# Copies of the key tiles issued from ScalarE's queue, and the key transposes at a higher scheduling priority

## The chip, the cores and the metric

The kernel runs on one core of one Trainium2 chip. The metric is the device time in microseconds (us) of one execution; lower is better. A core has five engines that run their own instruction streams side by side: PE (TensorE, matrix multiplications and transposes), DVE (VectorE), ACT (ScalarE), POOL (GpSimd) and SP (SyncE, which here only issues transfers). Transfers (DMAs) are issued by an instruction on one of these streams and then run by themselves; an instruction that needs the data waits for a semaphore. Each stream is in order: an instruction that waits holds back all that stand behind it on its engine.

## The reference

One step of a two-layer streaming encoder, on 1024 new frames of one stream ("prompt", 8 tiles of 128 rows) and on 8 running streams of 16 frames ("sample", one tile of 128 rows), model width 1024, 16 query heads and 4 key heads of 64.

```python
for layer in range(DEPTH):                       # DEPTH = 2
    if layer < N_LAYERS_A:                       # layer 0, mixer A
        qp, kp, vp = project_a(hp, g_attn[layer], w_qkv_a[i], g_q_a[i], g_k_a[i])
        ap = band_attention_prompt(qp, kp, vp, LEFT_CHUNKS_A, alibi_fn, sink_a[i])
        ...                                      # the same for the sample, with cached keys
        hp = hp + ap @ w_o_a[i]
    else:                                        # layer 1, mixer B
        kb_p, vb_p = shared_kv(hp, g_kv, w_kv, g_k_b)
        qp = project_q_b(hp, g_attn[layer], w_q_b[j], g_q_b[j])
        ap = band_attention_prompt(qp, kb_p, vb_p, LEFT_CHUNKS_B, rel_fn, None)
        ...
        hp = hp + ap @ w_o_b[j]
    hp = hp + mlp(hp, g_mlp[layer], w_up[layer], w_down[layer])
    hs = hs + mlp(hs, g_mlp[layer], w_up[layer], w_down[layer])
```

project_a and shared_kv are an RMS norm, a projection and an RMS norm of each key head; attention is softmax(q k^T + bias) v over the own 64-row chunk and 2 (A) or 8 (B) chunks before it; the MLP is relu(x w_up)^2 w_down.

## The kernel before

Every fp32 matrix product is made of values that are split in two, hi and lo, and three matmuls (L186 to L188 in the projections, L147 to L149 in the output projection, L715 to L717 in the MLP). A split is a cast on ACT (L109, hi) and a subtraction on DVE (L115, lo).

In each layer an attention part is followed by an output projection and an MLP. The attention part handles the 8 prompt tiles t = 0..7 and the sample tile ST. For one tile these steps are called, each a small function in the code:

- X(t): the tile's input is loaded from DRAM, x<-xd in layer 1 (L1319, issued by SP).
- N(t): eight PE transposes (ps_n, L179), the split into hh and hl, the sum of squares on ACT (junk, L170). For most tiles hh and hl are also stored to DRAM (hTd, L1349); R(t) brings them back later for the other projection chunks (hh<-hTd, hl<-hTd, L1358). There is one pair of buffers for hh and hl.
- K1(t): the key and value projection, and its finish kv_stage1 (kw by ACT L252 and L253, the norm, ks on DVE).
- K2(t): k_transpose. Two PE transposes of ks into a PSUM tile ps_q (L229), a split into the key tile KT[:, t, :, 0] (two casts on ACT, two subtractions on DVE, of 64 partitions each), and then two DMAs (L282 and L283, 64 partitions and 128 KB each) that copy the two halves, exchanged, into KT[:, t, :, 1]. Scores take a query's upper or lower half against a key tile in the same partitions, so both copies are needed (matmuls L349 in layer 0, L400 and L468 in layer 1).
- Q1(t, nb) and Q2(t, nb): the query projection, its norm (qn and qr on ACT, L195 and L196), four PE transposes of qr into ps_q (L229), and the split into qT (L109 and L115).
- Scores, softmax (L354 to L385 in layer 0, L428 to L440 and L486 in layer 1), transposes of p (ps_tr, L293), their split pth and ptl, and the product with the values (ps_pv, L300 and L301).

Eight prompt tiles in two layers make 16 calls of k_transpose with copies, and so 32 DMAs.

The code calls these steps in the order of a plan, but the order in which they stand on each engine is set by the framework's scheduler: it takes the instructions by priority (those recorded earlier have the higher one) against its own simulation of the engines. `with self.tc.high_priority(n)` raises the priority of what is recorded inside it by n. Both the instruction stream of ACT and that of SP are a result of that scheduling, and so are buffers' reuse and who waits for whom. Nothing is written out by hand here (cfg's `order` is empty).

Each DMA, when it ends, raises one of eight semaphores (DMAHW0 to DMAHW7), which all hardware DMAs of SP and ACT take in turn; before a DMA is issued, its engine waits until the earlier DMA on the same semaphore has landed.

Of the kernel before, what the change touches and what calls it, by code (L numbers as in the profile page):

```python
# [8 lines left out]
F32 = mybir.dt.float32  # L9
# [66 lines left out]
class Build:  # L76
# [197 lines left out]
    def k_transpose(self, ks, dst):  # L274
        a, b = slice(0, 64), slice(64, 128)
        pt = self.transpose_pairs(ks, 2)
        even, odd = dst[0][:, 0::2], dst[0][:, 1::2]
        self.split(even[a], even[b], pt[a])
        self.split(odd[b], odd[a], pt[b])
        if len(dst) > 1:  # L280
            if self.kd:
                self.nc.sync.dma_start(dst[1][a].bitcast(F32), dst[0][b].bitcast(F32))  # L282
                self.nc.sync.dma_start(dst[1][b].bitcast(F32), dst[0][a].bitcast(F32))  # L283
            else:
                even, odd = dst[1][:, 0::2], dst[1][:, 1::2]
                self.split(even[b], even[a], pt[a])
                self.split(odd[a], odd[b], pt[b])
# [324 lines left out]
    def wo_phase(self, layer, sx, x8, wo):  # L612
        nc = self.nc
        with ExitStack() as st:
# [6 lines left out]
            def O(t, z):  # L621
# [8 lines left out]
                if t in self.wo_done:  # L630
                    return
                with self.tc.high_priority(WO_PRIO) if len(osp) < 2 else nullcontext():
                    load_o(t, z)
# [5 lines left out]
            def load_o(t, z):  # L639
                o = work.tile([P, 4, P], F32, tag=f"o{z}", name="o")  # L640
                self.load_halves(layer, 1, t, o, second, nc.vector)
                oh = work.tile([P, 4, P], F32R, tag=f"oh{z}", name="oh")
                ol = work.tile([P, 4, P], F32R, tag=f"ol{z}", name="ol")
                self.split(oh, ol, o)
                osp[t] = oh, ol
# [73 lines left out]
    def behind(self, a, b):  # L719
        self.tc.add_manual_dep(b.ins, a.ins.name, AFTER, reason="order")  # L720

# [540 lines left out]
    def attention(self, layer):  # L1262
# [17 lines left out]
        with ExitStack() as st:  # L1280
# [24 lines left out]
            hts, qTs, qss, kss, probs, oTs, xr = {}, {}, {}, {}, {}, {}, {}  # L1305
# [74 lines left out]

            def K2(t):
                if t < NT:
                    self.k_transpose(kss.pop(t), [self.KT[:, t, :, v] for v in range(2)])
                else:
                    kt8 = self.rawp.tile([P, KV, P], F32R, tag="raw", name="kt8")
                    self.k_transpose(kss.pop(t), [kt8])
                    nc.sync.dma_start(self.kT8d[layer], kt8.bitcast(F32))
# [203 lines left out]
            spill(0)  # L1591
            run(Q1(0, 0))
            K2(0)
            spill(1)
            run(Q1(1, 0, "s"))
            Q2(0, 0)
            K2(1)
            spill(ST)
            run(Q1(ST, 0, "s"))
            K2(ST)  # L1600
            X(2)
            N(2)
# [57 lines left out]
            for s in range(2 * NT):  # L1660
# [8 lines left out]
                a, b, c, d = cfg["up"]  # L1669
# [72 lines left out]
]  # L1742

WO_PRIO = 600
AFTER = mybir.DependencyInfo(mybir.DependencyClass.NoSync, mybir.DependencyReason.DATA)
EARLY = (300, 150, 110, 90)
WO_ORDER = [[0, 4, 1, 5, 2, 6, 3, 7, ST], [0, 4, 1, 5, 6, 2, 7, 3, ST]]
# [51 lines left out]
```

## Time and profile before

| | us |
|---|---|
| median of 3 runs | 2405.27 |
| lowest and highest | 2404.04, 2407.24 |
| span of the profiled execution | 2399.3 |
| PE busy | 2320.4 (97% of the span) |
| DVE busy | 1626.3 (68%) |
| ACT busy | 1217.9 (51%) |
| POOL busy | 535.6 (22%) |

The profiled execution has a span, from its first to its last recorded instruction; no other time is listed for it, so it is the span that stands beside the median of the runs, which is 6.0 us longer. A row of a timeline gives the start, the duration, the engine, the line, the operation, the tile written and the tile read, and in brackets how long the engine sat idle before it and what ended that wait. "SPq" and "ACTq" are the issues of DMAs on SP and ACT. The attention part of layer 0 lies at about 43 to 283 us of the span, that of layer 1 at about 1184 to 1391 us.

### The profile page before, as it was taken

How to read it: one execution, taken by the hardware profiler on the slowest of the kernel's cores; microseconds unless marked ns; L12 is line 12 of the kernel's file. 1: busy time of each engine (PE TensorE's matmuls, PEld its weight loads, DVE VectorE, ACT ScalarE, POOL GpSimd, SP SyncE). 2: the span in 40 equal slices, each digit the busy share in tenths (PEclk: the TensorE clock that was granted, in tenths of full speed). 3: DMA queues.
4: the chain of work that ended last, by engine and by line, in shares of the span. 5: the costliest groups of instructions: out<-in, count | busy, mean ns of one | idle time of the engine just before them, and what ended most of it. 6: DMA issues, size and time to landing. Idle time of an engine off the chain costs nothing.

```text
span 2399.3 us, 33421 instructions
## 1 busy us (share of the span) xinstructions
PE 2320.4 (97%) x11621; PEld 1935.5 (81%) x11621; DVE 1626.3 (68%) x3002; ACT 1217.9 (51%) x2423; POOL 535.6 (22%) x828
## 2 busy tenths in 40 slices
PE   7998999899999999999999999998999999999999
PEld 6786877788888888888777788887888888888887
DVE  6687786755655777776567877877655555776674
ACT  4676675555555433232267666665655555333321
POOL 3343332312112100000333434344211211000000
PEclk9998999999999999999999999999999999999999
DMA  7345546244433874342743555555434435744332
GB/s 244 122 127 168 171 156 200 95 155 158 145 128 141 323 245 146 117 141 99 237 149 111 188 161 173 173 169 174 138 127 145 154 137 200 278 140 158 112 116 114
DMA packets 218457, 385.88 MB, mean 161 GB/s; under 512 B 50408, under 2 KB 125104, under 8 KB 211120
## 3 DMA queue, kind: packets, MB, share of 16 engines
q1 hardware_dynamic: 195136, 307.16, 39.0%
q0 software_dynamic: 21776, 71.84, 7.7%
q10 hardware_dynamic: 1376, 4.74, 0.5%
q8 instruction: 92, 1.51, 0.3%
q14 instruction: 77, 0.63, 0.1%
HBM read 246.47 MB, written 136.14 MB: 159 GB/s over the span
## 4 chain that ended last, share of the span: by engine, by line
PE 82%; DMA 7%; DVE 5%; ACT 2%; issue 2%; POOL 1%; SPq 1%; ACTq 0%; DVEq 0%; POOLq 0%
PE ps_x L715 9%; PE ps_x L717 9%; PE ps_x L716 9%; PE ps_y L717 7%; PE ps_y L716 7%; PE ps_y L715 7%; PE ps_mm L186 3%; PE ps_mm L188 3%; PE ps_mm L187 3%; PE ps_tr L293 2%; PE ps_mm L147 2%; PE ps_mm L149 2%; PE ps_mm L148 2%; PE ps_s L717 1%; PE ps_s L716 1%
## 5 line engine op out<-in xcount | busy, mean ns | idle before, releaser
L109 ACT CAST w<-r 128x2048 fp32r<-128x2048 f32 x56 | 107.1, 1913 | 322.9 <-PE ps_y L717 212.1
L715 PE MATMUL ps_x<-w,s 128*128 128x512 f32 x512 | 199.5, 390 | 2.7 <-DVE hc L854 2.1
L717 PE MATMUL ps_x<-w,s 128*128 128x512 f32 x512 | 199.4, 389 | 0.0
L716 PE MATMUL ps_x<-w,s 128*128 128x512 f32 x512 | 199.2, 389 | 0.0
L186 PE MATMUL ps_mm<-w,hh 128*128 128x512 f32 x432 | 175.0, 407 | 13.8 <-ACT kw L253 5.1
L188 PE MATMUL ps_mm<-w,hl 128*128 128x512 f32 x432 | 174.3, 403 | 1.7 <-DMA hl<-hTd 1.4
L187 PE MATMUL ps_mm<-w,hh 128*128 128x512 f32 x432 | 172.5, 400 | 0.7 <-DVE w L159 0.7
L109 ACT CAST s<-s 128x2048 fp32r<-128x2048 f32 x56 | 107.1, 1913 | 117.9 <-DMA s<-hd 108.6
L115 DVE TENSOR_TENSOR w<-r,w 128x2048 fp32r<-128x2048 f32 x56 | 128.2, 2290 | 51.9 <-ACT w L109 51.9
L715 PE MATMUL ps_x<-sx,w 128*128 128x512 f32 (+1 forms) x408 | 157.8, 387 | 4.6 <-ACT hc L834 2.7
L1021 DVE TENSOR_TENSOR x<-ps_y,x 128x512 f32<-128x512 f32 x136 | 92.3, 687 | 101.1 <-PE ps_y L717 101.0
L717 PE MATMUL ps_x<-sx,w 128*128 128x512 f32 (+1 forms) x408 | 154.1, 378 | 0.0
L716 PE MATMUL ps_x<-sx,w 128*128 128x512 f32 (+1 forms) x408 | 154.1, 378 | 0.0
L109 ACT CAST w<-ru 128x512 fp32r<-128x512 f32 (+1 forms) x160 | 110.0, 708 | 85.3 <-PE ps_y L716 32.0
L717 PE MATMUL ps_y<-w,s 128*128 128x512 f32 x384 | 149.5, 389 | 0.0
L716 PE MATMUL ps_y<-w,s 128*128 128x512 f32 x384 | 149.4, 389 | 0.0
L715 PE MATMUL ps_y<-w,s 128*128 128x512 f32 x384 | 149.4, 389 | 0.0
L115 DVE TENSOR_TENSOR s<-s 128x2048 fp32r<-128x2048 f32 x56 | 128.1, 2287 | 26.5 <-ACT s L109 26.5
L115 DVE TENSOR_TENSOR ptl<-ps_tr,pth 128x512 fp32r<-128x512 f32 x180 | 122.6, 685 | 24.8 <-ACT pth L109 19.0
L115 DVE TENSOR_TENSOR w<-ru,w 128x512 fp32r<-128x512 f32 (+1 forms) x160 | 126.6, 793 | 10.9 <-ACT w L109 10.8
L109 ACT CAST pth<-ps_tr 128x512 fp32r<-128x512 f32 x180 | 104.8, 594 | 47.9 <-PE ps_tr L293 39.3
L115 DVE TENSOR_TENSOR wq<-ru,wq 128x1024 fp32r<-128x1024 f32 x32 | 39.7, 1240 | 131.9 <-ACT wq L109 131.9
(280 smaller groups left out, 6573.3 us busy)
## 6 DMA issues: line engine op xcount, KB each, us to landing
s<-hd SPq DMA_DIRECT2D x56, 1024.0 KB, 4.7
ru<-in_w_up SPq DMA_DIRECT2D x64, 512.0 KB, 3.9
r<-in_w_down SPq DMA_DIRECT2D x32, 1024.0 KB, 5.7
hd<-hc POOLq DMA_DIRECT2D x128, 256.0 KB, 2.7
hd<-hs POOLq DMA_DIRECT2D x96, 256.0 KB, 2.5
x<-xd SPq DMA_DIRECT2D x41, 512.0 KB, 4.6
o<-oTd SPq DMA_DIRECT2D x52, 256.0 KB, 4.1
hTd<-hh SPq DMA_DIRECT2D x36, 256.0 KB, 4.5
```

What stands on the lines that cost most here:

```text
L109: a = nc.scalar.copy(hi, src)
L115: return a, e.tensor_tensor(lo, src, hi.bitcast(F32), ALU.subtract)
L147: nc.tensor.matmul(ps, oh[:, k, :], w[:, 0, k, nn], start=(k == 0), stop=False)
L148: nc.tensor.matmul(ps, oh[:, k, :], w[:, 1, k, nn], start=False, stop=False)
L149: nc.tensor.matmul(ps, ol[:, k, :], w[:, 0, k, nn], start=False, stop=(k == 3))
L186: nc.tensor.matmul(ps, a, w[:, 0, k, :], start=(k == 0), stop=False)
L187: nc.tensor.matmul(ps, a, w[:, 1, k, :], start=False, stop=False)
L188: nc.tensor.matmul(ps, b, w[:, 0, k, :], start=False, stop=(k == KC - 1))
L715: a = mm(ps, ah, bh, start=first, stop=False, skip_group_check=True)
L716: mm(ps, ah, bl, start=False, stop=False, skip_group_check=True)
L717: return a, mm(ps, al, bh, start=False, stop=last, skip_group_check=True)
L1021: tt(xs[t][:, N[n]], ps, xs[t][:, N[n]], ALU.add)
```

## The change

The two copies in k_transpose are issued by ACT (nc.scalar) instead of SP (nc.sync), and the call of k_transpose for the prompt tiles stands inside high_priority(100), which raises the priority of its transposes, of its casts and subtractions, and of its two DMAs. Lines after L1382 stand one lower in the changed code.

```diff
@@ k_transpose
         if len(dst) > 1:
             if self.kd:
-                self.nc.sync.dma_start(dst[1][a].bitcast(F32), dst[0][b].bitcast(F32))
-                self.nc.sync.dma_start(dst[1][b].bitcast(F32), dst[0][a].bitcast(F32))
+                self.nc.scalar.dma_start(dst[1][a].bitcast(F32), dst[0][b].bitcast(F32))
+                self.nc.scalar.dma_start(dst[1][b].bitcast(F32), dst[0][a].bitcast(F32))
@@ attention part
             def K2(t):
                 if t < NT:
-                    self.k_transpose(kss.pop(t), [self.KT[:, t, :, v] for v in range(2)])
+                    with self.tc.high_priority(K_PRIO):
+                        self.k_transpose(kss.pop(t), [self.KT[:, t, :, v] for v in range(2)])
@@
 WO_PRIO = 600
+K_PRIO = 100
```

Both parts change what the scheduler makes of the attention parts: instructions change places on all five engines between 48 and 282 us and between 1184 and 1390 us of the old span, and at a few places between 346 and 373 us. The MLPs and most of the output projections keep their order. SP loses 32 rows and ACT gains them.

Three places follow. The first is on SP at the start of layer 1, where x<-xd_113 is the input of a prompt tile; the two pairs of KT copies are those of tiles 0 and 1.

```order
 L265 DMA out<-v_11058 128x256
 L1349 DMA hTd_128<-hl 128x512
-L282 DMA KT<-KT 64x4x128
-L283 DMA KT<-KT 64x4x128
 L263 DMA out<-kw 128x256
-L282 DMA KT<-KT 64x4x128
 L1319 DMA x<-xd_113 128x1024
-L283 DMA KT<-KT 64x4x128
-L1387 DMA kT8d_158<-kt_11465 128x512
+L1388 DMA kT8d_158<-kt_11465 128x512
 L1319 DMA x<-xd_114 128x1024
```

Between the store of kw and the load of x<-xd_113 nothing is left on SP.

On ACT at the same place, before, the casts of tile 1's keys and queries alternate:

```order
L195 ACTIVATE qn<-ps_mm 128x512
L196 COPY qr<-ps_mm 128x512
L109 CAST qT<-ps_q 64x4x128
L109 CAST KT<-ps_q 64x2x128
L109 CAST qT<-ps_q 64x4x128
L109 CAST KT<-ps_q 64x2x128
L195 ACTIVATE qn<-ps_mm 128x512
```

And after:

```order
L195 ACTIVATE qn<-ps_mm 128x512
L196 COPY qr<-ps_mm 128x512
L109 CAST KT<-ps_q 64x2x128
L109 CAST qT<-ps_q 64x4x128
L109 CAST KT<-ps_q 64x2x128
L282 DMA KT<-KT 64x4x128
L283 DMA KT<-KT 64x4x128
L109 CAST qT<-ps_q 64x4x128
L195 ACTIVATE qn<-ps_mm 128x512
```

The second cast of qT now stands behind both issues.

The second place is on ACT in layer 0 at tile 1 (about 52 us), before:

```order
L109 CAST qT<-ps_q 64x4x128
L109 CAST KT<-ps_q 64x2x128
L195 ACTIVATE qn<-ps_mm 128x512
L170 ACTIVATE junk,xssq<-x 128x1024
L109 CAST qT<-ps_q 64x4x128
L109 CAST kt_644<-ps_q 64x2x128
L109 CAST KT<-ps_q 64x2x128
```

And after:

```order
L109 CAST KT<-ps_q 64x2x128
L196 COPY qr<-ps_mm 128x512
L109 CAST qT<-ps_q 64x4x128
L109 CAST KT<-ps_q 64x2x128
L282 DMA KT<-KT 64x4x128
L109 CAST qT<-ps_q 64x4x128
L195 ACTIVATE qn<-ps_mm 128x512
L109 CAST kt_644<-ps_q 64x2x128
L170 ACTIVATE junk,xssq<-x 128x1024
L283 DMA KT<-KT 64x4x128
```

The long junk instruction has moved behind the second cast of qT, and one DMA issue has come ahead of that cast.

The third place is on PE in layer 0 near tile 6 (about 175 us), where hh_2409 and hl_2410 are a pair that R(t) brings back from DRAM, before:

```order
L188 MATMUL ps_mm_2313<-w_352,hl_2061 128x512
L349 MATMUL ps_s_2339<-KT_214,qT_2235 128x256
L574 MATMUL ps_utp_2320<-identr_66,sp_2165 128x128
L575 MATMUL ps_utp_2320<-identr_66,sp_2165 128x128
L293 MATMUL ps_tr_2326<-identr_66,p_2034 128x128 x4
L300 MATMUL ps_pv_2358<-pth_2288,VS_215 128x512
L301 MATMUL ps_pv_2358<-ptl_2289,VS_215 128x512
L576 MATMUL ps_utp_2320<-identr_66,pn_2163 128x128
L186 MATMUL ps_mm_2581<-w_2396,hh_2409 128x512
```

And after, where the same ps_utp group stands:

```order
L186 MATMUL ps_mm_2581<-w_2396,hh_2409 128x512
L349 MATMUL ps_s_2422<-KT_214,qT_2235 128x256 x4
L187 MATMUL ps_mm_2581<-w_2396,hh_2409 128x512
L188 MATMUL ps_mm_2581<-w_2396,hl_2410 128x512
L574 MATMUL ps_utp_2320<-identr_66,sp_2165 128x128
L575 MATMUL ps_utp_2320<-identr_66,sp_2165 128x128
L293 MATMUL ps_tr_2326<-identr_66,p_2034 128x128
L576 MATMUL ps_utp_2320<-identr_66,pn_2163 128x128
L293 MATMUL ps_tr_2326<-identr_66,p_2034 128x128 x3
```

The whole projection of 24 matmuls into ps_mm_2581, which needs the reload, has come ahead of the group.

The DMAs on ACT and SP take the eight semaphores in one common turn, so an issue on ACT can have to wait for a transfer of SP. In the changed program most of the 32 issues share theirs with a store or a small load from the tile before; in layer 0 the second issue for tile 7 shares it with the load hl<-hTd that SP issued at 194.45 us of the old span, and behind that issue on ACT stand the softmax steps L382 and the casts of pth.

## The prediction

> **What bounds the kernel now.** I read the page's first lines, then the stretches of the span, then the waits of PE, SP and ACT, and then the timelines of the places that the change touches.
>
> ```profile
> span 2399.3 us, 33421 instructions
> PE 2320.4 (97%) x11621; PEld 1935.5 (81%) x11621; DVE 1626.3 (68%) x3002; ACT 1217.9 (51%) x2423; POOL 535.6 (22%) x828
> ```
>
> PE is busy for 97% of the span: the kernel is bound by matmuls, and no more than 79 us of idle PE are left in all. What a change of queues and of order can win is part of that, and the half-speed clock that follows some of it. The view of busy time by stretch tells where it lies (columns: stretch, its length, busy time and instructions of PE, PEld, DVE, ACT and POOL, then the mean granted PE clock, the DMA share and GB/s).
>
> ```profile
> 43.00:283.00 240.00, 221.79 (x1194) 182.98 (x1193) 185.36 (x599) 162.12 (x472) 94.56 (x163) 0.96 0.46 146
> 480.00:1184.00 704.00, 700.40 (x3278) 585.08 (x3277) 445.75 (x507) 293.38 (x367) 80.79 (x144) 1.00 0.48 167
> 1184.00:1391.00 207.00, 193.72 (x1032) 157.49 (x1032) 157.47 (x439) 137.53 (x373) 84.30 (x112) 0.99 0.52 158
> 55.00:60.00 5.00, 4.78 (x17) 3.58 (x16) 4.23 (x13) 4.38 (x12) 0.89 (x2) 0.66 0.69 228
> 1209.00:1214.00 5.00, 4.97 (x25) 4.21 (x26) 2.46 (x12) 4.02 (x14) 2.74 (x7) 0.66 0.53 164
> ```
>
> The MLP of layer 0 (480 to 1184) leaves 3.6 us idle and is not changed. The two attention parts, where the change acts, leave 240 - 221.79 = 18.2 and 207 - 193.72 = 13.3 us. ACT works 162.12 + 137.53 of 447 us there, 67%, so it has room, but it is no empty engine. The last two rows are short stretches behind two waits of PE: the clock is 0.66 over 5 us, so each holds 0.34 x 5 = 1.7 us of lost speed beside the wait itself.
>
> **Part 1: SP loses 32 issues.** The operations' own views and SP's waits:
>
> ```profile
> L282 SPq DMA_DIRECT2D KT<-KT x16: 597/617/707, 42.2 to 1377.2; - x16
> L655 ACTq DMA_DIRECT2D xd<-x x9: 326/327/373, 407.4 to 1673.5; - x9
> SPq L282 <- ACT KT L109: 20.4, 8, 5.7
> ```
>
> A copy costs SP 0.617 us of issue (minimum, median and maximum in ns), so 32 x 0.617 = 19.7 us leave SP. SP bounds nothing by its issues; the 19.7 us are worth nothing by themselves. What counts is the third row: SP stood 20.4 us in 8 waits at the first copy, for ACT's cast of KT, the longest 5.7 us, and whatever was queued behind stood too. I looked for the place where that reached PE.
>
> ```profile
> 1197.79 0.35 SPq L263 DMA_DIRECT2D out<-kw  x1
> 1203.91 0.60 SPq L282 DMA_DIRECT2D KT<-KT  x1
> 1204.60 0.55 SPq L1319 DMA_DIRECT2D x<-xd  x1
> 1205.25 0.60 SPq L283 DMA_DIRECT2D KT<-KT  x1
> 1203.87 1.91 PE L400 MATMUL ps_sn<-KT,qT 128*128 128x128 f32 x12
> 1208.90 1.20 PE L179 MATMUL ps_n<-identr,x 128*128 128x128 f32 x8 [3.13 <-DMA x<-xd]
> 1204.60 4.26 DMA x<-xd
> 1203.03 0.58 ACT L109 CAST qT<-ps_q 64x512 fp32r<-64x512 f32 x1 [0.55 <-DVE qT L115]
> ```
>
> SP issues a store at 1197.79, stands until 1203.91 for the cast, and only then issues the load of x, which lands 4.26 us later (the row of the chain) at 1208.9. PE had nothing else: 3.13 us idle, and 1.7 us by the clock, 4.8 us in all. After the change the load follows the store at once: issue at about 1198.2, landing at 1202.5, before PE is through with its scores. But on ACT the second cast of qT (1203.03 before) now stands behind two issues, 2 x 0.617 = 1.2 us, and the scores L400 need it. So the wait for x goes, and about 1.4 us of waiting for qT takes its place: 3.13 - 1.4 = 1.7 us of idle time saved, and the 1.7 us of clock, since waits of about 1 us elsewhere are not followed by a slow clock. Term: **-3.4** (bounds -4.8, if the scores are not late, and 0, if they are late by as much as x was).
>
> The Trainium skill (DMA: Bandwidth & Descriptors, Issuing engines are not separate DMA queues) says that transfers started by different engines run on the same 16 DMA engines, and that starting them from several engines saves only the issuing engine's time, usually small. By it alone this term would be about 0 and the time 2403.3. The row speaks against it here: what delayed x was not the 0.617 us of an issue but 5.7 us of an in-order queue standing at a wait.
>
> **Part 2: the order in layer 0, tile 1.**
>
> ```profile
> 52.02 1.05 ACT L170 ACTIVATE junk<-x 128x1024 bf16<-128x1024 f32 x1
> 53.18 0.58 ACT L109 CAST qT<-ps_q 64x512 fp32r<-64x512 f32 x1
> 53.80 0.69 DVE L115 TENSOR_TENSOR qT<-ps_q,qT 64x512 fp32r<-64x512 f32 x1 [0.26 <-ACT qT L109]
> 54.63 0.63 PE L229 MATMUL ps_q<-identr,qr 128*128 128x128 f32 x4 [1.94 <-DVE qT L115]
> 64.94 0.49 PE L186 MATMUL ps_mm<-w,hh 128*128 128x512 f32 x1 [0.69 <-ACT kw L253]
> ```
>
> PE waits 1.94 us for a PSUM buffer that the cast and the subtraction of qT have to read first; the cast stood behind junk (1.05 us, and 0.1 to the next). With junk behind it, the cast starts 1.15 us earlier, less 0.6 for the issue that stands ahead of it now: 0.55. The wait shrinks to about 1.4 us, and the 1.7 us of slow clock behind it go: **-2.3** (bounds 0, if ACT stands at the issue for as long as junk took, and -3.6, if the whole wait goes). The wait of 0.69 us at 64.94 goes too, since the scores on which DVE was then late are taken ten matmuls earlier: **-0.7** (bounds -0.7 and 0).
>
> **Part 3: the reloads in layer 0.**
>
> ```profile
> 175.93 0.33 SPq L1434 DMA_DIRECT2D oTd<-oT  x1
> 176.34 6.25 DMA hh<-hTd
> 178.53 0.33 PE L574 MATMUL ps_utp<-identr,sp 128*128 128x128 f32 x1 [3.23 <-DVE w L159]
> 180.37 0.41 PE L576 MATMUL ps_utp<-identr,pn 128*128 128x128 f32 x1
> 182.73 0.77 PE L186 MATMUL ps_mm<-w,hh 128*128 128x512 f32 x1 [1.95 <-DMA hh<-hTd]
> 202.11 0.47 PE L186 MATMUL ps_mm<-w,hh 128*128 128x512 f32 x1 [2.38 <-DMA hh<-hTd]
> 203.38 0.79 PE L188 MATMUL ps_mm<-w,hl 128*128 128x512 f32 x1 [0.57 <-DMA hl<-hTd]
> ```
>
> Before, PE idles 3.23 us, works 2.25 us (178.53 to 180.78), idles 1.95 us more for the reload, and at the next reload 2.38 + 0.57: 8.13 us. After, the projection stands ahead of that 2.25 us group, so PE idles through to the landing. The reload is issued some 0.9 us sooner, since the store at 175.93 and a copy are no longer ahead of it: the first idle time is 3.23 + 2.25 + 1.95 - 0.9 = 6.5 us. The group then fills 2.25 us of the second: 2.95 - 2.25 = 0.7. In all 7.2, so **-1.0** (bounds +2.25, if the group fills nothing, and -4, if both landings come sooner by 1.5 us each).
>
> **Part 4: layer 1, tile 3.**
>
> ```profile
> 1257.08 3.61 DMA KT<-KT
> 1260.83 0.47 PE L468 MATMUL ps_s<-KT,qT 128*128 128x512 f32 x1 [1.75 <-DMA KT<-KT]
> ```
>
> Scores wait 1.75 us for the copy itself, whose landing takes 3.61 us. Issued by ACT straight behind its cast it is hardly earlier, as it still needs DVE's half; but the scheduler puts other matmuls ahead of it. **-0.5** (bounds -1.75 and 0).
>
> **Part 5: ACT's 32 issues.** No copy was issued by ACT before; the nearest row, another DMA, is 0.327 us, and the same copy on SP is 0.617, so ACT gains 10.5 to 19.7 us of issue; I take the latter, the same transfer. The cover is ACT's idle third. Where it fails, the next cast or exponential is 1.2 us late for a tile, and PE waits if that came last. How often that is, PE's waits in the two attention parts tell (total, times, longest):
>
> ```profile
> PE ps_pv L300 <- ACT pth L109: 3.1, 3, 1.9
> PE ps_mm L186 <- ACT qr L196: 1.5, 2, 1.0
> PE ps_mm L186 <- ACT kw L253: 0.7, 1, 0.7
> PE ps_mm L186 <- ACT qr L196: 1.0, 1, 1.0
> PE ps_sf L400 <- ACT p L437: 1.0, 4, 0.3
> ```
>
> Only three waits on ACT are of 1 us or more (1.9 and the two of 1.0). Tile 1 of both layers is in the terms above. Of the other 14 tiles I let two pay in full, 2 x 1.23: **+2.5** (bounds 0, all covered, and 32 x 0.617 = 19.7, none).
>
> **Sum.** -3.4 - 2.3 - 0.7 - 1.0 - 0.5 + 2.5 = -5.4 us on the span of 2399.3: 2393.9. The median of the runs is 6.0 us above that span, which I take as unchanged: 2405.3 - 5.4 = **2399.9 us**. A measurement of this kernel tells about 0.2%, 4.8 us, from no change, so the forecast is only just on the faster side.
>
> **Rivals.**
> *ACT pays back what SP wins.* For it: ACT's casts and exponentials feed PE through PSUM buffers, and 11 waits on ACT stand in the rows above. Against: ACT is idle a third of the time. If five tiles pay instead of two, 5 x 1.23 = 6.2, the sum is -1.7: 2403.6, no change.
> *The slow clock stays.* If the clock does not come back with the shorter waits, the terms at 1208.9 and 54.63 lose 1.7 us each, and the sum is -2.0: 2403.3, no change. Against it: both stretches at 0.66 lie straight behind the waits. The Trainium skill (TensorE: Matmul & The Clock Gate, Part 1: The HAM clock gate) gives this rival its rule: half clock comes after an idle window of about 3.4 us, free-running. Waits of 1.94 and 3.13 us would then be too short to cause it; the two rows at 0.66 say that they sufficed, so I give it little.
> *Slower: ACT stands at the issues.* A copy on ACT must wait for its cast, for DVE's half and for the DMA that used its semaphore last, and ACT is in order, so the wait holds back casts and exponentials. The place to look is tile 7 of layer 0, where the second issue shares its semaphore with the reload of hl:
>
> ```profile
> 194.45 8.89 DMA hl<-hTd
> 199.27 0.60 SPq L283 DMA_DIRECT2D KT<-KT  x1
> ```
>
> It landed at 203.3, while the copy was issued at 199.27: 4.1 us of standing for ACT. PE waits for that reload anyway at 202 to 203.4, so once alone it costs little. If it happens at three tiles where PE has no such cover, 3 x 4.1 = 12.3 more, the sum is +6.9: 2412.2. It decides from two such tiles on (-5.4 + 8.2 = +2.8). Against it: most of these semaphores belong to stores that were issued several us before.
> *The order moves without use.* The edits do change the order, so "nothing happens" is not open; that the moves cost as much as they win (part 3 at +2.25 and part 2 at 0) gives -3.4 - 0.7 + 2.25 - 0.5 + 2.5 = +0.2, no change.
>
> **How the numbers follow.** The forecast 0.44; ACT pays back 0.16; the clock stays 0.05; moves without use 0.15; ACT stands at its issues 0.20. A tenth of the forecast's share lies above -4.8, where it is no change, and some of the three middle cases lies below it, which I set equal: faster 0.45, no change 0.36, slower 0.19. The low end of the range is the sum with part 1 at -4.8, part 2 at -3.6 - 0.7, part 3 at -1 and 4 at -0.5 and with ACT free, -10.6, and 2 us more of part 3: 2392.7, rounded down; the high end takes in half of the slower case, +6: 2411. I end at 2392 to 2411. The forecast's own range is 2394 to 2403.
>
> **What the new profile would show.** Part 1: x<-xd issued straight behind the kw store, no wait of ps_n for x near 1209, and no stretch at 0.66 behind it; instead at most 1.5 us of waiting for qT at the scores. Part 2: the wait for ps_q near 54.6 at 1.5 us or less, with the clock near 1. Part 3: one wait for hh of about 6.5 us near 182, under 1 us at the next. Part 5: "ACTq L282" and "L283" of about 0.62 us each, ACT's issues standing little. I am wrong if ACTq's waits add up to tens of us, if PE's waits on ACT in the two attention parts grow by more than 5 us, or if the clock falls to half at new places.

## The result, and the profile after

| | before | changed |
|---|---|---|
| median (10 runs each), us | 2404.65 | 2412.14 |
| lowest and highest, us | 2397.1, 2410.63 | 2408.96, 2419.72 |
| span of the profiled execution, us | 2399.3 | 2408.5 |

The ratio of the changed kernel to the one before is 1.0033, with a 95% interval of 1.002 to 1.0046: 0.33% or about 8 us slower. The forecast was 2399.9 us.

The stretches of the changed kernel, in the view of busy time by stretch (columns as above):

```profile
43.00:283.00 240.00, 223.73 (x1221) 184.89 (x1220) 189.34 (x611) 165.28 (x486) 96.01 (x165) 0.97 0.47 149
1184.00:1391.00 207.00, 187.20 (x977) 152.41 (x976) 150.90 (x425) 131.23 (x360) 79.57 (x106) 0.98 0.50 152
1204.00:1209.00 5.00, 3.19 (x17) 3.05 (x17) 3.62 (x15) 3.38 (x7) 1.18 (x1) 0.72 0.24 56
1209.00:1214.00 5.00, 5.00 (x26) 3.85 (x25) 4.44 (x17) 4.98 (x22) 3.15 (x8) 0.94 0.67 212
1355.00:1360.00 5.00, 3.71 (x11) 3.03 (x12) 4.88 (x11) 4.05 (x12) 3.49 (x4) 0.66 0.79 284
1373.00:1378.00 5.00, 4.85 (x18) 4.27 (x19) 2.32 (x8) 0.86 (x2) 2.58 (x4) 0.66 0.49 176
55.00:60.00 5.00, 4.73 (x15) 3.51 (x14) 3.88 (x9) 3.74 (x10) 2.28 (x3) 0.66 0.96 316
```

PE does the same 11,621 matmuls, and in all it is as busy as before (2320.9 us against 2320.4). In the attention part of layer 0 its idle time fell from 18.2 to 16.3 us; in that of layer 1 it grew from 13.3 to 19.8 us within the same 207 us, in which PE got through 977 matmul records instead of 1032.

Where the time goes is seen best if the start of PE's n-th instruction in one trace is set against that of the other. (The order differs by at most 44 places, so the figures wobble by a microsecond or two.)

```
before, us    260   483   1124   1195   1256   1332   1373   1446   1708
after-before -4.9  -3.2   -2.3   -1.1   -0.9   +1.3   +8.9   +7.6   +9.2
```

The changed kernel leads by 2 to 5 us from 260 us to the end of layer 0, loses a little at the start of layer 1, and loses 8 us between 1332 and 1373, in the last third of layer 1's attention part. There three long waits of PE are new (timeline of PE in the changed kernel; the second figure is the duration, in brackets stands the wait and what ended it):

```profile
1344.02 0.50 PE L186 MATMUL ps_mm<-w,hh 128*128 128x512 f32 x1 [2.38 <-ACT kw L253]
1356.29 0.70 PE L186 MATMUL ps_mm<-w,hh 128*128 128x512 f32 x1 [1.96 <-ACT ub L570]
1373.15 0.52 PE L186 MATMUL ps_mm<-w,hh 128*128 128x512 f32 x1 [2.39 <-DMA hh<-hTd]
```

The clock is full behind the first of them (1.00 from 1345 to 1350) and at 0.66 over the 5 us behind each of the other two, rows 1355 and 1373 above, which is 1.7 us of lost speed each time. Before, it was full from 1332 to the end of this attention part.

At the same place before, the projection waited 0.40 us for kw:

```profile
1337.30 0.62 PE L400 MATMUL ps_sf<-KT,qT 128*128 128x384 f32 x2 [0.22 <-ACT p L437]
1340.15 0.43 PE L549 MATMUL ps_us<-kb,qu 128*128 128x288 f32 x2
1341.98 0.50 PE L186 MATMUL ps_mm<-w,hh 128*128 128x512 f32 x1 [0.40 <-ACT kw L253]
```

What made that wait longer is seen on ACT, before:

```profile
1337.75 0.37 ACT L109 CAST KT<-ps_q 64x256 fp32r<-64x256 f32 x1
1338.14 0.47 ACT L245 ACTIVATE VS<-ps_mm,rx 128x256 fp32r<-128x256 f32 x1
1340.91 0.48 ACT L251 ACTIVATE vsb<-ps_mm,rx 128x256 f32<-128x256 f32 x1
1341.53 0.40 ACT L253 ACTIVATE kw<-ps_mm 128x256 f32<-128x256 f32 x1
```

And in the changed kernel:

```profile
1338.41 0.37 ACT L109 CAST KT<-ps_q 64x256 fp32r<-64x256 f32 x1
1340.14 0.47 ACT L245 ACTIVATE VS<-ps_mm,rx 128x256 fp32r<-128x256 f32 x1
1341.11 0.37 ACT L109 CAST KT<-ps_q 64x256 fp32r<-64x256 f32 x1
1342.94 0.47 ACT L251 ACTIVATE vsb<-ps_mm,rx 128x256 f32<-128x256 f32 x1 [0.86 <-DVE VS L246]
1343.57 0.40 ACT L253 ACTIVATE kw<-ps_mm 128x256 f32<-128x256 f32 x1
```

In the old order the cast of VS (L245) stands ahead of three softmax steps, and DVE's half of it (L246) is done in time. In the new order it stands behind them and has one more cast of KT behind it; DVE does its half only at 1342.50, and ACT stands 0.86 us for it before it gets to kw. Counted from the scores ahead (1337.30 before, 1338.10 in the changed kernel), kw is there 1.24 us later. PE's rows in between are almost the same in both orders (the sample's scores, L549, are missing in the new one), and it is through with them 0.74 us sooner. The two make the 1.98 us by which the wait grew.

The places of the prediction, in the changed kernel (SP and PE timelines):

```profile
1195.48 0.34 SPq L263 DMA_DIRECT2D out<-kw  x1
1195.91 0.38 SPq L1319 DMA_DIRECT2D x<-xd  x1
1203.50 0.66 PE L400 MATMUL ps_sn<-KT,qT 128*128 128x128 f32 x4 [0.53 <-DVE qT L115]
1205.97 1.38 PE L400 MATMUL ps_sn<-KT,qT 128*128 128x128 f32 x6 [1.81 <-DVE qT L115]
54.54 0.50 PE L186 MATMUL ps_mm<-w,hh 128*128 128x512 f32 x1 [1.23 <-ACT hh L109]
180.87 0.55 PE L349 MATMUL ps_s<-KT,qT 128*128 128x256 f32 x1 [9.04 <-DMA KT<-KT]
1258.51 0.48 PE L468 MATMUL ps_s<-KT,qT 128*128 128x512 f32 x1 [0.37 <-DMA KT<-KT]
```

The load of x follows the store at once, and PE does not wait for x any more, but 0.53 + 1.81 us for qT. The slow clock has not gone with the wait: it stands behind the waits for qT now (0.72 over 1204 to 1209, where it was 1.00 before). In layer 0 a new wait of 9.04 us for the key copy stands where two waits of 3.23 and 1.95 us stood.

### The profile page after: what moved, and what is told of

Its sections match the earlier page's. It is cut to its first block, busy times and chain, and to the rows that moved or that the text cites. A ratio compares the mean times of both kernels' runs of the same rounds, so it can differ in the third digit from the quotient of the medians.

```text
span 2408.5 us, 33389 instructions
## 1 busy us (share of the span) xinstructions
PE 2320.9 (96%) x11621; PEld 1937.1 (80%) x11621; DVE 1626.7 (68%) x3002; ACT 1216.2 (50%) x2423; POOL 537.5 (22%) x828
## 4 chain that ended last, share of the span: by engine, by line
PE 79%; DMA 7%; DVE 7%; ACT 4%; issue 2%; POOL 1%; SPq 1%; ACTq 0%; DVEq 0%; POOLq 0%
PE ps_x L715 9%; PE ps_x L717 9%; PE ps_x L716 9%; PE ps_y L717 7%; PE ps_y L716 7%; PE ps_y L715 7%; PE ps_mm L186 3%; PE ps_mm L188 3%; PE ps_mm L187 3%; PE ps_tr L293 2%; PE ps_mm L147 2%; PE ps_mm L149 1%; PE ps_mm L148 1%; PE ps_s L717 1%; PE ps_s L716 1%
```

## The experiments

The question was which of three things costs: the queue (issues in ACT's in-order stream), the priority, or the order that the scheduler makes of either. All ratios are to the kernel before, run beside it; brackets are 95% intervals. In these series the kernel before had medians of 2399 to 2405 us, so between series the ratios are compared, not the times.

**By layer.** Both parts of the change in one layer alone; the other layer is issued in its old order, instruction for instruction.

```diff
+                (self.nc.scalar if layer in K_LAYERS else self.nc.sync).dma_start(dst[1][a]...
+                    with (self.tc.high_priority(K_PRIO) if layer in K_LAYERS else nullcontext()):
+K_LAYERS = (0,)     # e3_layer0;  (1,) in e4_layer1
```

> Both parts of the change in layer 0 alone; layer 1 is issued in the old order. In the two traces the same count of TensorE instructions is reached 4.9 us sooner after layer 0's attention part and 2.3 us sooner at the end of its MLP, then later in layer 1. If the loss belongs to layer 1 alone: about 2402 us (before 2404.65), -2 to -5. If the copies on ScalarE's queue cost wherever they stand, and layer 0's gain was an accident of one profile: 2405 to 2409.

> Both parts of the change in layer 1 alone; layer 0 is issued in the old order. If the two layers add up, with layer 1's share read from the traces as 9.25 + 2.3 = 11.6 us: about 2416 us. If layer 1 suffers only from what layer 0 hands on (other transfers in flight, other buffers): 2405 to 2409.

Measured: layer 0 alone 0.9988 [0.9978, 0.9998], 2400.79 us; layer 1 alone 1.0046 [1.0029, 1.0063], 2415.05 us. The two add up to +0.34%, which is the whole. The loss belongs to layer 1; layer 0 gains a little, less than its lead in the one trace said. The trace of e4_layer1, where layer 0 has the old order, is 5.6 us ahead of the profile before at 260 us: most of that lead was this one profile.

**By part.** The queue without the priority, and the priority without the queue; each gives the scheduler's own order.

```diff
 # e1_queue: as the change, without
-                    with self.tc.high_priority(K_PRIO):
 # e2_prio: as the change, with
-                self.nc.scalar.dma_start(dst[1][a]...
+                self.nc.sync.dma_start(dst[1][a]...
```

> The copies on ScalarE's queue, without the higher priority. The scheduler makes an order of its own from it. Theory 'standing': ScalarE, which is in order, stands at the copies' issues until their halves and semaphores are ready, and this is what costs: then it is slow here too, 2410 to 2416 us. Theory 'priority': key casts pulled ahead of casts and exponentials that TensorE needs sooner are what costs: then 2400 to 2406.

> The higher priority alone, the copies on SyncE as before. Theory 'standing': no cost on ScalarE is left, 2400 to 2406 us, and SyncE stands at its copies as before. Theory 'priority': 2410 to 2416 us.

Measured: queue alone 1.0073 [1.0057, 1.0088], 2419.19 us; priority alone 1.0008 [0.9997, 1.0018], 2405.11 us. The priority is harmless, and beside the queue it gives back about half of what the queue costs. But in both kernels the order is different too, so this does not yet say whether ACT's standing or the order costs.

**Queue and order apart.** In the next kernels the order of every engine is written out and held: an edge that sets issue order alone is put between each two neighbours of an engine. The old order with the copies on ACT (h1_held), each pair straight behind its second key cast; and the new order with the copies on SP (h2_sp), each at the place that it had in time.

```diff
     with tile.TileContext(nc, **TC_KW) as tc:
         Build(tc, ins, outs).run()
+        freeze(tc, nc)      # add_manual_dep(b, a.name, AFTER) for neighbours a, b of the order
 # h1_held: old order                          # h2_sp: new order
-                self.nc.sync.dma_start(...     -                self.nc.scalar.dma_start(...
+                self.nc.scalar.dma_start(...   +                self.nc.sync.dma_start(...
```

> The old order of every engine, held by order edges, and only the 32 copies moved from SyncE's stream to ScalarE's, each pair straight behind its second key cast. Theory 'issue': the copies' time and waits in ScalarE's in-order stream are the loss; then about 2410 to 2415 us (before 2403.4 to 2404.7). Theory 'order': the loss is in the new order of casts and matmuls, and the queue by itself costs little and frees SyncE for the load of x at the start of layer 1; then 2399 to 2405.

> The order of the changed kernel on every engine, held by order edges, and only the 32 copies put back on SyncE, each at the place in its stream that it had in time on ScalarE in the profile. Theory 'issue': the loss goes, 2400 to 2405 us. Theory 'order': it stays, 2409 to 2414.

| | copies on SP | copies on ACT |
|---|---|---|
| old order | 1 | 1.0097 [1.0081, 1.0112] |
| new order | 1.0025 [1.001, 1.004] | 1.0033 [1.002, 1.0046] |

Neither theory alone is right. In the old order the queue costs 0.97%, 23 us. In the new order it costs 0.08%, 2 us, which is within the error. The new order by itself, with SP's copies, costs 0.25%, 6 us. So most of the changed kernel's loss is there without a copy on ACT. The wait for kw is too: with the copies on SP it is 2.38 us again, behind the same 0.85 us of ACT standing for VS:

```profile
1341.97 0.47 ACT L251 ACTIVATE vsb<-ps_mm,rx 128x256 f32<-128x256 f32 x1 [0.85 <-DVE VS L246]
1343.05 0.50 PE L186 MATMUL ps_mm<-w,hh 128*128 128x512 f32 x1 [2.38 <-ACT kw L253]
```

Holding an order was not run by itself, without any change; h4_xfirst below, the old order held with one row moved, is at 1.0012 [0.9998, 1.0025], so nothing points to holding as a cost of its own. The order that the scheduler made for e1_queue was not held with its copies on SP, so how its 0.73% divide between queue and order is open.

What the queue does in the old order is seen on ACT (timeline of ACT in h1_held, two tiles of layer 0):

```profile
160.18 0.37 ACT L109 CAST KT<-ps_q 64x256 fp32r<-64x256 f32 x1
160.58 0.60 ACTq L282 DMA_DIRECT2D KT<-KT  x1
162.14 0.60 ACTq L283 DMA_DIRECT2D KT<-KT  x1
162.78 0.58 ACT L326 COPY pvt<-ps_pv 64x512 f32<-64x512 f32 x1 [2.23 <-DVE nm L359]
183.35 0.60 ACTq L282 DMA_DIRECT2D KT<-KT  x1
189.72 0.60 ACTq L283 DMA_DIRECT2D KT<-KT  x1
190.36 0.58 ACT L109 CAST qT<-ps_q 64x512 fp32r<-64x512 f32 x1 [7.04 <-DVE KT L115]
```

The second copy needs DVE's half of the split, so ACT issues one copy, stands 0.96 us (in the second tile 5.77 us) and issues the other. From the end of ACT's instruction ahead to the end of the issue, the 32 copies take 34.7 us of ACT in all.

**Standing or issuing.** The same kernel with 23 of the 32 copies one to six instructions further back on ACT; the other nine stay where they were (the expectation says one to eight rows, for all).

```diff
 # h3_late, ACT's held order at a tile
  L109 CAST KT<-ps_q
-L282 DMA KT<-KT
-L283 DMA KT<-KT
  L326 COPY pvt<-ps_pv
+L282 DMA KT<-KT
  L109 CAST pth<-ps_tr
  L570, L571 ...
+L283 DMA KT<-KT
```

> As the kernel with the old order held and the copies on ScalarE (1.0097), but each of the 32 copies stands one to eight ScalarE rows further back, behind the instruction that ran when SyncE issued it in the old profile, so that its half and its cast are ready and another instruction can be in flight. If ScalarE's standing at issues whose halves are not ready is most of the 23 us: 2408 to 2414 us. If the 0.6 us of each issue is: 2420 or more.

Measured: 1.0014 [1.0003, 1.0026], 2406.81 us, faster than either theory had it. Six sevenths of the queue's cost are gone though each issue still takes 0.60 us; the sum of 34.7 us has become 12.7. That sum is no price, though: counted in the same way it is 22.6 us in the changed kernel, where the queue costs 2 us, and 15.0 in e1_queue. What ACT loses counts only where PE comes to wait for it. The row of ACT shows how an issue can cost nothing (timeline of ACT in h3_late):

```profile
152.10 0.37 ACT L109 CAST KT<-ps_q 64x256 fp32r<-64x256 f32 x1
152.50 0.58 ACT L326 COPY pvt<-ps_pv 64x512 f32<-64x512 f32 x1
152.50 0.60 ACTq L282 DMA_DIRECT2D KT<-KT  x1
154.04 0.31 ACT L571 ACTIVATE pn<-sp,li 128x32 f32<-128x32 f32 x1
154.06 0.60 ACTq L283 DMA_DIRECT2D KT<-KT  x1
```

The copy is issued while the instruction ahead of it runs: both start at 152.50.

**The place of the new order's loss.** The changed kernel, order and queue, up to a time of its profile, and the old order behind that. The two kernels differ in what stands between 1332 and 1349, with tile 6's two copies, which are on ACT in the second. Cut at 1332 us (g1_cut), and at 1349 us (g3_cut).

```diff
+        freeze(tc, nc)      # new order for what started before the cut, old order for the rest
 # copies behind the cut on SP: tiles 6 and 7 of layer 1 (g1_cut), tile 7 (g3_cut)
```

> The order and queue of the changed kernel up to 1332 us of its profile, held by order edges; behind it the old order, with the copies of layer 1's tiles 6 and 7 on SyncE. If the loss sits in the new order of that last stretch of layer 1's attention (6 to 9 us between 1335 and 1358 in two profiles): 2400 to 2404 us. If it comes from what stands ahead and only shows there: 2408 to 2413.

> As the kernel cut at 1332 us (1.0000, where the changed kernel is 1.0033), but the order of the changed kernel is kept up to 1349 us of its profile and the old order stands only behind that; the copies of tile 7 alone are on SyncE. If the loss of the last stretch is made by the wait for kw near 1344 (2.4 us and the slow clock behind it): 1.002 to 1.003. If it is made by what stands behind 1349 (casts of the output weights ahead of those of p, a late reload of hh): about 1.000.

Measured: 1.0000 [0.9989, 1.0012] for the cut at 1332, 1.0028 [1.0017, 1.004] for the cut at 1349. With the changed kernel at 1.0033, nearly all of the loss, 0.28% or 7 us, is made by what stands in these 17 us. PE in the two kernels (stretch 1330 to 1350 of each, columns as above, g1_cut first; then PE's wait for kw in each):

```profile
1330.00:1350.00 20.00, 16.87 (x89) 12.87 (x88) 17.59 (x46) 12.64 (x37) 9.36 (x13) 1.00 0.48 152
1339.06 0.50 PE L186 MATMUL ps_mm<-w,hh 128*128 128x512 f32 x1 [0.41 <-ACT kw L253]
```

```profile
1330.00:1350.00 20.00, 16.22 (x76) 12.77 (x75) 14.64 (x37) 10.62 (x32) 7.10 (x11) 0.91 0.50 153
1345.87 0.50 PE L186 MATMUL ps_mm<-w,hh 128*128 128x512 f32 x1 [2.38 <-ACT kw L253]
```

The wait for kw is 0.41 us in the one and 2.38 us in the other, the same two values as in the kernel before and the changed one, and in g3_cut the clock falls behind the longer one (0.91 over the stretch). In the same 20 us PE gets 13 matmul records less done. The two queued copies of tile 6 are not what makes the wait, since h2_sp has it without them. Which single row of the order makes it was not tried apart; that it is the later cast of VS is read from the timelines of ACT. How 2 us of waiting become 7 is shown in part: the traces have it in more waits and slow stretches behind the first, at 1356 and 1373 in the changed kernel and at 1360 in g3_cut, but not in the same places. And one trace proves little here: g1_cut and g3_cut have the same order up to 1332, and there one is 6.5 us ahead of the other.

**Part 1 of the prediction alone.** The old order held, and one row of SP moved.

```diff
 # h4_xfirst, SP's held order at the start of layer 1
  L263 DMA out<-kw
+L1319 DMA x<-xd_113
  L282 DMA KT<-KT
-L1319 DMA x<-xd_113
  L283 DMA KT<-KT
```

> The old kernel with its order held and a single row of SyncE moved: the load of x at the start of layer 1 stands ahead of tile 1's first copy instead of behind it. By the prediction's first step the wait of 3 to 4 us and the slow clock behind it go: 2399 to 2402 us. If another wait takes its place: 2403 to 2405.

Measured: 1.0012 [0.9998, 1.0025], 2403.23 us: no gain. The trace shows the load at its new place and the gain going away (h4_xfirst, SP and PE):

```profile
1200.03 0.38 SPq L1319 DMA_DIRECT2D x<-xd  x1
1206.93 0.60 SPq L282 DMA_DIRECT2D KT<-KT  x1
1208.66 1.06 PE L179 MATMUL ps_n<-identr,x 128*128 128x128 f32 x8
1211.16 0.66 PE L400 MATMUL ps_sn<-KT,qT 128*128 128x128 f32 x4 [1.01 <-ACT p L440]
1212.35 0.63 PE L229 MATMUL ps_q<-identr,qr 128*128 128x128 f32 x4 [0.52 <-DVE li L447]
1214.07 0.79 PE L186 MATMUL ps_mm<-w,hh 128*128 128x512 f32 x1 [1.09 <-ACT hh L109]
```

x is loaded 6.9 us ahead of the copy and PE doesn't wait for it; 1.01 + 0.52 + 1.09 us for ACT and DVE stand next, and the matmuls behind them are slow again.

**A version that beats both.** The change in layer 0 and, in layer 1, for tiles 0 and 1 alone (b1_first); and its order held with its 20 copies on SP (h5_b1sp).

```diff
 # b1_first
+                    with (self.tc.high_priority(K_PRIO) if layer == 0 or t < 2 else nullcontext()):
 # and nc.scalar under the same condition;  h5_b1sp: freeze with b1_first's order, nc.sync for all
```

> Both parts of the change in layer 0 and, in layer 1, for tiles 0 and 1 alone; behind them layer 1 is issued in the old order. From the traces of the two single-layer kernels, whose start of layer 1 differs by 2 to 3 us in favour of the new order and whose tiles 3 to 7 differ by 11 us in favour of the old one: 0.9988 less 0.001, about 2398 us. If the new order's start is no gain on the median: 2401.

> The order of the fastest kernel so far (the change in layer 0 and in tiles 0 and 1 of layer 1, 0.9975), held, with its 20 copies on SyncE instead of ScalarE, each at its place in time. If the order alone makes it faster: 0.997 to 0.9985. If the freed SyncE does: 0.9995 to 1.001.

Measured: 0.9975 [0.9963, 0.9986], 2399.11 us, and 0.9978 [0.9966, 0.9991], 2394.37 us (beside a before of 2399.21 in that series). Both are faster than the kernel before by 0.22 to 0.25%, and the second has no copy on ACT at all: the gain is the order's, not the queue's.

## Why the prediction was wrong

**The order elsewhere, taken at nothing: the step that failed.** I read the order at the places where the old kernel had waits and summed what would become of these. The loss is at a place where the old kernel had a wait of only 0.40 us: what stands between 1332 and 1349 makes 7 of the 8 us (g1_cut, g3_cut). A list of old waits can only show gains; that 1376 of PE's instructions change places is an equal chance for new waits, and in the sum it had no term. In its place stand the wait for kw, 2.38 us instead of 0.40, as ACT gets to kw later, and the waits and slow stretches behind it. Two of the prediction's own signs tell it: the clock falls to half at new places (1356 and 1373), and PE's waits on ACT grow by more than 5 us, in layer 1 alone from 3.5 to 9.3. In h2_sp, with no copy on ACT, they are 8.5: it is the order that makes PE wait for ACT, and not the queue.

**The slow clock, taken back twice.** Parts 1 and 2 each count 1.7 us of clock, 3.4 of the 5.4 us that the sum forecasts, and neither came back. This was the rival "the slow clock stays", which got 0.05.

**Part 5, ACT's issues.** I priced the issues by their own 0.617 us and let two of 14 tiles pay: +2.5 us. The issue time was right (0.598 us on ACT), and in the new order the queue does cost about that (2 us between h2_sp and the changed kernel). The term was about right for this order, but not its bounds: the price of the same 32 issues runs from 3 us (h3_late) to 23 us (h1_held) in the old order, above my upper bound of 19.7. That bound counted issue time alone, and left out the standing for the other half of the data. I had this standing in a rival, but put it on a semaphore shared with a reload and on tile 7 of layer 0. In the changed kernel ACT issues that copy within 1.5 us of the other. The rival's time, 2412.2, is close to the measured 2412.14 by accident; its mechanism is not what costs in the changed kernel.

**Part 1, -3.4.** The wait for x went, as forecast, but 2.3 us of waiting for qT came instead of my 1.4, and the slow clock only moved: 1209 to 1214 rose from 0.66 to 0.94, and 1204 to 1209 fell from 1.00 to 0.72, in all the same 1.7 us. In the pair of traces the part is worth 0.8 us. By itself the step gives nothing on the median (h4_xfirst excludes -3.4 us, 0.14%).

**Part 2, -2.3 and -0.7.** The wait for ps_q at 54.63 and that at 64.94 are gone; in place of the first, PE waits 1.23 us for hh at 54.54, so that the idle time is near the forecast 1.4 by luck. But the clock of 55 to 60 us is 0.66 as before: the 1.7 us of the slow clock, most of the term, did not come back. My ground, that waits of about 1 us are not followed by a slow clock, does not hold: here 1.23 us were. In b1_first and h5_b1sp the same wait of 1.23 us, at 55.6 and 55.4, is not followed by one, and the wait of 2.38 us is in g3_cut but not in the changed kernel. So the length of the wait alone does not decide it. The rule of the Trainium skill (TensorE: Matmul & The Clock Gate, Part 1: The HAM clock gate) that half clock comes after an idle window of about 3.4 us fits this place no better.

**Part 3, -1.0.** I had PE idle for 6.5 us for the reload of hh, and 0.7 us at the next. It idles 9.04 us, for the key copy itself, and not at the next. The copy, 128 KB, was issued at 171.72 by ACT, 0.75 and 0.25 us behind the issues of hh and hl on SP, and landed 9.0 us later, where the median of the copies is 2.4. That agrees with the sentence of the Trainium skill (DMA: Bandwidth & Descriptors, Issuing engines are not separate DMA queues) that transfers from different engines interleave on the same DMA engines: another queue gave this copy no way past the reload. Issued by SP in the same order it took 7.6 us (h2_sp). Against 8.13 us before, the part is +0.9 in this pair of traces.

**Part 4, -0.5.** The wait for the copy fell from 1.75 to 0.37 us, and a wait of 1.15 us for kw came 3 us later: nearly even.

The runs divide the 8 us in two ways. By layer, layer 0 gives -2.9 us (parts 2 and 3 and all else there) and layer 1 +11. By cause, the new order costs 6 us and the queue in it 2, which is within the error.

## What to carry to other kernels

Before moving a transfer to a compute engine's queue, look for what its issue has to wait for there: an issue that stands for another engine's half stops everything behind it, and a few rows further back it costs next to nothing (0.97% against 0.14% here). When an edit also makes a scheduler reorder, separate the two by holding the order on one side; here no run shows a gain from the queue, and the order made most of the changed kernel's loss and the gain of b1_first. And give the reordering a term of its own in the forecast, at places without old waits too: ask of each split whether its first half still comes early enough for the other engine to finish the second.

## What the runs showed of the hardware

A DMA issue on ACT runs beside an ACT instruction that is in flight (both at 152.50 in h3_late), and where ACT has nothing in flight, some 0.63 us of its stream are lost to one. The same copy costs 0.598 us of issue on ACT and 0.617 on SP. A 128 KB copy took 9.0 us to land beside 512 KB reloads, against a median of 2.4. In the 14 traces, every stretch of slow clock between 60 us and the last 10 us of the span is at 0.5 and lasts 3.41 us or two or three times that, 1.7 us of lost speed for each 3.41. Equal waits of PE (1.23 us in five traces, 2.38 in four) are followed by one in some traces and not in others.
